# Residual block on one core: gate_up weights alone on SyncE's queue, first products one step apart, sums of h2 behind the last norm, second products out of other tiles

## The chip, the cores and the metric

One core of a Trainium2 chip runs the whole program. The metric is the device time of one execution in microseconds (us). TensorE (PE) multiplies, VectorE (DVE), ScalarE (ACT) and GpSimd (POOL) do the rest, and SyncE (SP) only issues transfers. Each engine works through its own instructions in order and waits where an operand or a buffer isn't ready. ACT, POOL and SP can each issue transfers, and an engine's transfers are issued in the order of its instructions: one that must wait holds up the ones behind it.

## What is computed

A residual block: a token mixer (attention with forgetting and a gated short convolution side by side), its output projection, then a feed-forward part. Each of the two is normed on the way in and on the way out. The sequence has 1024 rows, the model 1024 columns, the feed-forward part F = 2816 columns; all is float32.

```python
h = rmsnorm(x, norm_mix_pre)
m = mixer(h, w_in, b_f, conv_w, w_branch, w_out)   # ends in einsum(merged, w_out)
x = x + rmsnorm(m, norm_mix_post)
h = rmsnorm(x, norm_ffn_pre)
gu = einsum("bsd,df->bsf", h, w_gate_up)           # gate_up
g, u = split(gu, 2)
f = einsum("bsf,fd->bsd", silu(g) * u, w_down)     # down
x = x + rmsnorm(f, norm_ffn_post)
```

The change is at the seam between the first sum and gate_up.

## The kernel before

**Products.** A float32 operand is split into hi, a rounded copy that ACT makes, and lo, the remainder that DVE makes by a subtraction (`split`). A product `prod` of a block of weights with a block of rows is 4 steps over the inner dimension, each of three matmuls of 128x512 (hi with hi, lo with hi, hi with lo): 12 matmuls. The large products use a scheme of the Strassen kind, with seven block products instead of eight, in which sums of the blocks are made ahead (T1 to T4 of the rows, S1 to S4 of the weights).

**Output projection.** The eight row tiles of 128 go in four pairs i (PAIRS). For each, `first` and `second` were done ahead, and the loop does `p_s2`, `p_s1`, `p_s3`, `p_s4`, `p_a22`. Then `e_norm(i)` norms the result, adds the residual x (tiles `xt`, loaded by `load_xt` up to three tiles ahead), stores the sum in `x2_dram`, and norms it again for the feed-forward part. `e_turn(i)` transposes these two row tiles on PE into `um`: eight transposes of the first tile (it lies in a raw slot, or in `keep` for i = 3), then eight of the second (`tt`). The halves of `um` are split into the operands `hb[B11]` and `hb[B21]`.

**gate_up.** The columns go in 22 blocks f, each of one gate and one up block of 128 columns and seven products. For the first 11 (NPRE) the two products that need B11 and B21 alone, A11 times B11 and A12 times B21, are done early: `f_first(f)` loads a weight block (512 KB, tile `raw`), splits it, does the first product into a bank, copies it to p1, does the second into the same bank on top of it, copies that to a tile `s4`, and stores both in `pre_dram` by POOL's queue. For f = 0 `e_turn(2)` stands between the two, for f = 3 `e_turn(3)`. `h2_sums(sl)` makes T1 to T4 of a quarter of the columns of `um`: four subtractions, and four splits. It is called twice between the early blocks, and twice behind f = 4 and 5. A loop over all 22 blocks follows, in which `strassen` does the five products that are left of the first 11 and all seven of the others; `prep_rest` makes their S1 to S4, S4 by way of the tile `s4`.

**What sets the order.** The helper `InOrder` records each operation (so all have one line, 76, in the profile, and are told apart by tile names), and a scheduler orders them for each engine; `pinned` keeps some in the order of the code. Tiles come from rings: `raw` has 3 buffers, `hi` 4, `lo` 3, `s4` 1, `s4h` and `s4l` 2, `sx` 1, the tiles `c21`, `c12`, `c22` of pool `fp` 2 each; a new tile waits until the users of the buffer's last one are done. Three of the raw slots also hold the normed row tiles until they are transposed. On SP's queue stand the loads of xt, the stores to x2_dram and the loads of the gate_up weights, in one line. In the profile the bank of a product is `b` (in the order of instructions `b_` and a number, one for each block f), `x` is an operand of hb, `s` and `c` are the tiles by which results leave, `x_dram` is x2_dram.

Of the kernel before, what the change touches and what calls it, by code (L numbers as in the profile page):

```python
# [10 lines left out]
F32 = mybir.dt.float32  # L11
# [6 lines left out]
P = 128  # L18
# [4 lines left out]
NC = 512  # L23
# [16 lines left out]
NPRE = 11  # L40
# [6 lines left out]
def block_kernel(  # L47
# [16 lines left out]
    n1, n2 = slice(0, NC), slice(NC, S)  # L64
# [3 lines left out]
    class InOrder:  # L68
# [15 lines left out]
    nc = SimpleNamespace(  # L84
        **{e: InOrder(e) for e in engines}
    )
    x2d = x[0]
# [6 lines left out]
    def pool(name, bufs=1, side="left", space=None):  # L94
        kw = dict(name=name, bufs=bufs)
        if space is not DRAM:
            kw["reuse_waits"] = "tile"
        if space is not None:
            kw["space"] = space
        else:  # L100
            kw["side"] = side
        stack = ExitStack()
        ctx.callback(stack.close)
        return stack.enter_context(tc.tile_pool(**kw)), stack.close
# [4 lines left out]
    def add(o, a, b):  # L109
        nc.vector.tensor_tensor(o, a, b, op=ALU.add)  # L110

    def sub(o, a, b):
        nc.vector.tensor_tensor(o, a, b, op=ALU.subtract)
# [4 lines left out]
    def pinned(call, *names):  # L118

        was, strict[0] = strict[0], names  # L120
        call()
        strict[0] = was

    def copy(o, a):
        nc.scalar.activation(o, a, AF.Copy)
# [6 lines left out]
    def mm3(ps, a, b, start, stop, **kw):  # L132

        ah, al = a
        bh, bl = b
        nc.tensor.matmul(ps, ah, bh, start=start, stop=False, **kw)
        nc.tensor.matmul(ps, ah, bl, start=False, stop=False, **kw)
        nc.tensor.matmul(ps, al, bh, start=False, stop=stop, **kw)
# [8 lines left out]
    x2_dram = dpool.tile([S, D], F32, name="x2_dram")  # L147
# [6 lines left out]
    pre_dram = [dpool.tile([2, P, NC], F32, name=f"pre_dram{f}") for f in range(NPRE)]  # L154
# [47 lines left out]
    def z_tile(name, dt=F32, w=S):  # L202
        return zp.tile([P, S], dt, tag="z", name=name, bufs=2)[:, :w]
# [218 lines left out]
    def flat(t):  # L422
        return t.rearrange("p a b -> p (a b)")

    def kblk(t):
        return t.rearrange("p (a b) -> p a b", b=P)

    def wtile(tag, bufs, dt=F32, shape=(P, KT, P)):
        return wpool.tile(list(shape), dt, tag=tag, name=tag, bufs=bufs)

    def raw_t():
        return wtile("raw", 3)
# [7 lines left out]
    def s4_t():  # L440
        return wtile("s4", 1, F32, (P, 4, P))
# [57 lines left out]
    def bank(psp, name):  # L499
        return psp.tile([P, NC], F32, tag="mm", name=name)  # L500

    def prod(ps, w, b, first):
        (ah, al), (bh, bl) = w, b
        kw = {} if first else dict(skip_group_check=True)
        for k in range(4):
            mm3(
                ps,
                (ah[:, k, :], al[:, k, :]),
                (bh[:, k, :], bl[:, k, :]),
                first and k == 0,  # L510
                k == 3,
                **kw,
            )

    def t_(tmp, name):
        return tmp.tile([P, NC], F32, tag=name, name=name)
# [52 lines left out]
    psm, psm_close = pool("psm", 6, space=PSUM)  # L569

    def wcols(c0):
        return win[:, c0 : c0 + P]
# [304 lines left out]
    for ij, (kind, j, _, _) in enumerate(jobs):  # L877
# [8 lines left out]
        if ij < 2:  # L886
# [6 lines left out]
            w = {**w, **prep_rest(wcols(jobs[ij][3]), r1)}  # L893
            if ij == 1:
                pairs.q.append(pairs.prep(*pairs.srcs.popleft()))
            _, c12, c21, c22 = strassen(w, h1b, psm, pp, p1, mid)
        elif ij < len(jobs) - 1:
# [5 lines left out]
            c11, c12, c21, c22 = strassen(pairs.get(), h1b, psm, pp, None, mid)  # L903
        else:
            w = pairs.get()
# [3 lines left out]
            c11, c12, c21, c22 = last_pair(w)  # L909
# [288 lines left out]
    psm, psm_close = pool("psm2", 8, space=PSUM)  # L1198
# [32 lines left out]
    def both(t):  # L1231
        return t[:, 0], t[:, 1]
# [75 lines left out]
    pk, pk_close = pool("pk", 4, space=PSUM)  # L1308
    psm, psm_close = pool("psm3", 4, space=PSUM)

    wy, wy_close = pool("wy", side="right")
    fe, fe_close = pool("fe", 2)
# [11 lines left out]
    def st2(name, bufs=2):  # L1324
        return ep.tile([P, 2], F32, tag=name, name=name, bufs=bufs)

    def scale2(ssq):
        return rms_scale(ssq, None, lambda n, w: st2(n), 2)
# [5 lines left out]
    sx = wtile("sx", 1)  # L1334
# [3 lines left out]

    def load_xt(st):
        xt = ep.tile([P, D], F32, name="xt") if st % 3 == 2 else z_tile("xt")  # L1340
        nc.sync.dma_start(xt, x2d[st * P : (st + 1) * P, :])
        return xt

    xts = deque(load_xt(st) for st in range(3))
# [58 lines left out]
    def e_norm(i):  # L1403
        qa = qas[i]
        add(qa, qa, qbs[i])
        rs = scale2(qa)
        tt = keeps[i], ep.tile([P, D], F32, tag="t", name="tt", bufs=1)
        xp = [xts.popleft() for _ in range(2)]
        ssq = st2("ssq")
        for e, parts in enumerate(  # L1410
            (((slice(0, D), keeps[i]),), ((n1, b1s[i]), (n2, c22s[i])))
        ):
            for ns, c in parts:
                nc.vector.scalar_tensor_tensor(
                    tt[e][:, ns], c, rs[:, e : e + 1], gpo[:, ns], op0=ALU.mult, op1=ALU.mult
                )
            add(xp[e], xp[e], tt[e])
            rows_ = slice((2 * i + e) * P, (2 * i + e + 1) * P)
            nc.sync.dma_start(x2_dram[rows_, :], xp[e])
            nc.scalar.activation(tt[e], xp[e], AF.Square, accum_out=ssq[:, e : e + 1])  # L1420
        rs = scale2(ssq)
        for e in range(2):
            nc.vector.scalar_tensor_tensor(
                tt[e], xp[e], rs[:, e : e + 1], gpr, op0=ALU.mult, op1=ALU.mult
            )
            if 2 * i + 3 + e < ST:
                xts.append(load_xt(2 * i + 3 + e))
        turned.append(tt)

    def e_turn(i):  # L1430
        for e in range(2):
            st = 2 * i + e
            ss = slice(st * P, (st + 1) * P)
            for q in range(2):
                tp = psm.tile([P, 4, P], F32, tag="mm", name="tp")

                def turns():
                    for k in range(4):
                        kt = 4 * q + k
                        nc.tensor.transpose(  # L1440
                            tp[:, k, :], turned[i][e][:, kt * P : (kt + 1) * P], ident
                        )

                pinned(turns, "tensor")
                copy(um[:, 4 * q : 4 * q + 4, ss], tp)
# [8 lines left out]
    for k in (0, 2):  # L1454
        w = ep.tile([P, D], F32, tag="t", name="wr", bufs=1)
        cut_wo(w, ((B22, 4 + k, n2), (B22, 5 + k, n2)))

    def f_src(f):
        return wgu[:, f * P : (f + 1) * P], wgu[:, FH + f * P : FH + (f + 1) * P]

    def f_first(f, p1=None, after=None):
        w, _ = prep_first(f_src(f)[0])
        b1 = bank(psm, "b1")
        prod(b1, w["A11"], hb[B11], True)
        if after is not None:
            after()
        if p1 is None:
            p1 = t_(fp, "c21")
        copy(p1, b1)
        prod(b1, w["A12"], hb[B21], False)  # L1470
        c11 = flat(s4_t())
        copy(c11, b1)
        nc.gpsimd.dma_start(pre_dram[f][0], p1)
        nc.gpsimd.dma_start(pre_dram[f][1], c11)

    h2b11 = x_tile(1)
# [6 lines left out]
    def h2_sums(sl):  # L1483
        a = slice(sl * P, (sl + 1) * P)
        b = slice(NC + sl * P, NC + (sl + 1) * P)
        b11, b12 = um[:, 0:4, a], um[:, 0:4, b]
        b21, b22 = um[:, 4:8, a], um[:, 4:8, b]
        u, w = wtile("sx", 1), raw_t()
        sub(u[:, LO], b12, b11)
        sub(u[:, UP], b22, u[:, LO])  # L1490
        sub(w[:, LO], b22, b12)
        sub(w[:, UP], b21, u[:, UP])
        for o, t in ((T2, u[:, UP]), (T1, u[:, LO]), (T3, w[:, LO]), (T4, w[:, UP])):
            split(hb[o][0][:, :, a], hb[o][1][:, :, a], t)
# [21 lines left out]
        e_norm(i)  # L1516
    hb.append(None)
    hb += [both(x_tile(n, p)) for n, p in ((0, wx), (3, wx), (4, wy), (5, wy))]
    def p1_of(f):
        return t_(fe, "c22")  # L1520

    f_first(0, p1_of(0), lambda: e_turn(2))
    f_first(1, p1_of(1))
    h2_sums(0)
    f_first(2, p1_of(2))
    h2_sums(1)
    f_first(3, p1_of(3), lambda: e_turn(3))
    ep_close()
    fe_close()
    psm_close()  # L1530
# [1 line left out]
    psm, psm_close = pool("psm4", 8, space=PSUM)  # L1532

    hc_pool, hc_close = pool("hc")
    fp, fp_close = pool("f", 2)
    hch = hc_pool.tile([P, 4, NC], F32R, name="hch")
    hcl = hc_pool.tile([P, 4, NC], F32R, name="hcl")
    hb[B22] = hch, hcl
    for f in range(4, NPRE):
        f_first(f)  # L1540
        if f < 6:
            h2_sums(f - 2)
        if f == 6:
            for sl in range(4):
                a = slice(sl * P, (sl + 1) * P)
                b = slice(NC + sl * P, NC + (sl + 1) * P)
                split(hch[:, :, a], hcl[:, :, a], um[:, UP, b])
# [25 lines left out]
    for f in range(NF):  # L1573
        if f < NPRE:
            p1 = t_(fp, "c21")
# [164 lines left out]
    p1, c22, c11, c12 = (quarter(s_) for s_ in (4, 6, 0, 2))  # L1740
# [109 lines left out]
```

## Time and profile before

| | us |
|---|---|
| median of three runs | 1347.06 |
| the three runs | 1346.71, 1347.06, 1347.97 |
| the profiled execution, its own time | 1347.87 |
| its span | 1346.1 |
| TensorE busy in it | 1319.9 |
| VectorE busy in it | 967.7 |
| ScalarE busy in it | 560.1 |
| GpSimd busy in it | 138.4 |

The span goes from the first to the last instruction; the execution's own time is 1.8 us longer. A row of a timeline has the start, the length, the engine, the operation with its tiles (out<-in) and shape, a count (xN, a run of like instructions told in one row), and in brackets the idle time before it with what ended it. Rows of different engines overlap, and on PE an instruction starts before the one ahead of it has ended, so lengths there don't add up. A row of waits has the engine and the tile that waited, what it waited for, the sum, the number and the longest. A row of transfers has the count, the size of one, and the median time from issue to landing. A stretch has its bounds, its length, the busy time of each engine that is listed (with the number of instructions), the granted clock of TensorE (1.00 is full), the share of the transfer engines and GB/s.

### The profile page before, as it was taken

The page shows a single profiled execution, that of the slowest core. Times are in us where ns is not written, and L with a number is a line of the kernel's source. Part 1 is how long each engine was busy: PE and PEld are TensorE (multiplying, and loading weights), DVE is VectorE, ACT ScalarE, POOL GpSimd, SP SyncE. Part 2 cuts the span into 40 slices and gives each one's busy share as a digit, 9 for nine tenths or more (in the row PEclk, how much of TensorE's full clock was granted, in tenths as well). Part 3 has the DMA queues.
Part 4 walks back from the last instruction along what each step waited for, and adds up shares of the span by engine and source line. Part 5 has one row for each costly group of instructions (what it writes and reads, how often), then busy time and mean ns, then how long its engine had stood idle before and what let it go on. Part 6 is the DMA issues. An engine that isn't in the chain of part 4 may idle for free.

```text
span 1346.1 us, 18023 instructions
## 1 busy us (share of the span) xinstructions
PE 1319.9 (98%) x6705; PEld 1089.5 (81%) x6705; DVE 967.7 (72%) x1530; ACT 560.1 (42%) x896; POOL 138.4 (10%) x264
## 2 busy tenths in 40 slices
PE   9999999999999999999999999999999999999997
PEld 7978888888887778788876778888888887888886
DVE  6975678775656767686798299897767766677585
ACT  6642222243355756514577233232222323444452
POOL 0001000010112112010001212220011101000000
PEclk9999999999999999999999999999999999999999
DMA  5334444455536444466247555652333326966541
GB/s 189 119 117 133 150 113 122 136 162 152 154 117 196 158 134 159 144 231 219 77 158 239 168 180 188 187 170 89 110 116 104 110 95 248 354 241 192 160 165 63
DMA packets 189738, 212.59 MB, mean 158 GB/s; under 512 B 11585, under 2 KB 137601, under 8 KB 189650
## 3 DMA queue, kind: packets, MB, share of 16 engines
q1 hardware_dynamic: 157890, 154.50, 36.7%
q0 software_dynamic: 14864, 48.55, 9.7%
q10 hardware_dynamic: 16896, 8.39, 2.1%
q8 instruction: 52, 0.85, 0.3%
q14 instruction: 36, 0.29, 0.1%
HBM read 151.83 MB, written 59.57 MB: 157 GB/s over the span
## 4 chain that ended last, share of the span: by engine, by line
PE 54%; DVE 5%; issue 2%; DMA 2%; ACT 1%; POOL 0%; DVEq 0%; SPq 0%; POOLq 0%; ACTq 0%
PE b L76 26%; PE pd L76 15%; PE pbb L76 3%; PE pba L76 2%; PE p L76 2%; PE po L76 1%; PE tps L76 1%; PE sp L76 1%; DMA raw<-in_w_gate_up_dram 1%; PE q L76 1%; DVE x L76 1%; DVE lo L76 1%; DVE raw L76 1%; DMA tk<-in_w_down_dram 1%; DVE tt L76 0%
## 5 line engine op out<-in xcount | busy, mean ns | idle before, releaser
L76 PE MATMUL b<-x,hi 128*128 128x512 f32 x1088 | 337.3, 391 | 3.4 <-ACT hi L76 1.7
L76 PEld LDWEIGHTS b<-x,hi 128*128 128x128 f32 x1088 | 203.1, 188 | 49.3 <-ACT c L76 4.4
L76 PE MATMUL b<-x,lo 128*128 128x512 f32 x544 | 211.9, 390 | 2.0 <-DVE lo L76 2.0
L76 DVE TENSOR_TENSOR c<-c,b 128x512 f32<-128x512 f32 x199 | 135.5, 682 | 68.6 <-PE b L76 61.3
L76 DVE TENSOR_TENSOR lo<-raw,hi 128x1024 fp32r<-128x1024 f32 (+1 forms) x93 | 112.0, 1204 | 72.4 <-PE b L76 59.4
L76 ACT ACTIVATE hi<-raw 128x1024 fp32r<-128x1024 f32 (+1 forms) x100 | 101.9, 1020 | 109.6 <-PE b L76 59.9
L76 ACT ACTIVATE hi<-sx 128x1024 fp32r<-128x1024 f32 (+1 forms) x43 | 44.8, 1042 | 187.6 <-PE b L76 150.9
L76 PEld LDWEIGHTS b<-x,lo 128*128 128x128 f32 x544 | 102.1, 188 | 24.3 <-DVE lo L76 2.8
L76 DVE TENSOR_TENSOR lo<-sx,hi 128x1024 fp32r<-128x1024 f32 (+1 forms) x43 | 51.5, 1198 | 30.8 <-PE b L76 30.1
L76 DVE TENSOR_TENSOR sx<-raw 128x512 f32<-128x512 f32 x78 | 53.6, 687 | 21.3 <-DMA raw<-in_w_gate_up_dram 9.5
L76 PE MATMUL pd<-hi 128*128 128x512 f32 x160 | 62.0, 391 | 0.6 <-ACT hi L76 0.6
L76 PE MATMUL pd<-hi,lo 128*128 128x512 f32 x160 | 62.3, 389 | 0.0
L76 PE MATMUL pd<-ghi 128*128 128x512 f32 x148 | 57.6, 389 | 0.0
L76 PE MATMUL pd<-glo,ghi 128*128 128x512 f32 x148 | 57.6, 389 | 0.0
L76 PE MATMUL pd<-ghi,glo 128*128 128x512 f32 x148 | 57.6, 389 | 0.0
L76 PE MATMUL b<-hT34h,hi 128*128 128x512 f32 x136 | 53.3, 392 | 0.6 <-DVE c L76 0.4
L76 PE MATMUL b<-hT34l,hi 128*128 128x512 f32 x136 | 52.9, 389 | 0.0
L76 PE MATMUL b<-hT34h,lo 128*128 128x512 f32 x136 | 52.9, 389 | 0.0
L76 PE MATMUL b<-hT12h,hi 128*128 128x512 f32 x136 | 52.9, 389 | 0.0
L76 PE MATMUL b<-hT12l,hi 128*128 128x512 f32 x136 | 52.9, 389 | 0.0
L76 PE MATMUL b<-hT12h,lo 128*128 128x512 f32 x136 | 52.9, 389 | 0.0
L76 ACT ACTIVATE s4h<-s 128x512 fp32r<-128x512 f32 x48 | 30.1, 628 | 52.8 <-DVE s L76 42.5
(410 smaller groups left out, 3026.5 us busy)
## 6 DMA issues: line engine op xcount, KB each, us to landing
raw<-in_w_gate_up_dram SPq DMA_DIRECT2D x55, 512.0 KB, 4.2
raw<-in_w_in_dram SPq DMA_DIRECT2D x35, 512.0 KB, 5.0
a_dramS<-um POOLq DMA_DIRECT2D x44, 256.0 KB, 2.9
a_dramA<-um POOLq DMA_DIRECT2D x33, 256.0 KB, 2.7
xt<-in_x_dram SPq DMA_DIRECT2D x16, 512.0 KB, 4.4
sg<-sg_dram SPq DMA_DIRECT2D x32, 256.0 KB, 3.1
x<-wo_dram SPq DMA_DIRECT2D x16, 512.0 KB, 8.7
graw<-a_dramS SPq DMA_DIRECT2D x14, 512.0 KB, 3.6
```

Of the source, the lines that this page charges most:

```text
L76: ins = getattr(self.engine, name)(*args, **kw)
```

## The change

The loads of xt and the stores of x2_dram go from SP's queue to GpSimd's. `f_first` is cut in two: `f_begin` loads, splits, does the first product, copies and stores it; `f_end` does the second, copies and stores that. The program begins block f + 1 before it ends block f. The early four copy their first product into the halves of `sx` and two `c22` tiles, and take their banks from the pool in which the output projection had `p1`. One raw slot is passed over before f = 2. `h2_sums` is called for f = 4 to 7, all behind the last norm, and has its `w` in a z tile rather than a raw slot. From f = 4 on the second product leaves by a `c12` tile (two buffers) and not by the `s4` tile (one). The split of the B22 operand (`hch`, `hcl`) moves from f = 6 to f = 8. What is computed stays the same.

```diff
     def load_xt(st):
-        nc.sync.dma_start(xt, x2d[st * P : (st + 1) * P, :])
+        nc.gpsimd.dma_start(xt, x2d[st * P : (st + 1) * P, :])
...
-            nc.sync.dma_start(x2_dram[rows_, :], xp[e])
+            nc.gpsimd.dma_start(x2_dram[rows_, :], xp[e])
...
-    def f_first(f, p1=None, after=None):
+    begun = {}
+
+    def f_begin(f, b1, p1):
         w, _ = prep_first(f_src(f)[0])
-        b1 = bank(psm, "b1")
         prod(b1, w["A11"], hb[B11], True)
-        if after is not None:
-            after()
-        if p1 is None:
-            p1 = t_(fp, "c21")
         copy(p1, b1)
+        nc.gpsimd.dma_start(pre_dram[f][0], p1)
+        begun[f] = w, b1
+
+    def f_end(f, c11):
+        w, b1 = begun.pop(f)
         prod(b1, w["A12"], hb[B21], False)
-        c11 = flat(s4_t())
         copy(c11, b1)
-        nc.gpsimd.dma_start(pre_dram[f][0], p1)
         nc.gpsimd.dma_start(pre_dram[f][1], c11)
...
-        u, w = wtile("sx", 1), raw_t()
+        u, w = wtile("sx", 1), kblk(z_tile("w"))
...
-    def p1_of(f):
-        return t_(fe, "c22")
-
-    f_first(0, p1_of(0), lambda: e_turn(2))
-    f_first(1, p1_of(1))
-    h2_sums(0)
-    f_first(2, p1_of(2))
-    h2_sums(1)
-    f_first(3, p1_of(3), lambda: e_turn(3))
+    sx = flat(wtile("sx", 1))
+    early = [sx[:, n1], sx[:, n2], t_(fe, "c22"), t_(fe, "c22")]
+
+    def begin_early(f):
+        if f == 2:
+            raw_t()
+        f_begin(f, pk.tile([P, NC], F32, tag="p1", name="b1"), early[f])
+
+    def end_early(f):
+        f_end(f, flat(s4_t()))
+
+    begin_early(0)
+    e_turn(2)
+    begin_early(1)
+    end_early(0)
+    begin_early(2)
+    end_early(1)
+    begin_early(3)
+    e_turn(3)
+    end_early(2)
+    end_early(3)
...
-    for f in range(4, NPRE):
-        f_first(f)
-        if f < 6:
-            h2_sums(f - 2)
-        if f == 6:
+    for f in range(4, NPRE + 1):
+        if f < NPRE:
+            f_begin(f, bank(psm, "b1"), t_(fp, "c21"))
+        if f > 4:
+            f_end(f - 1, t_(fp, "c12"))
+        if f < 8:
+            h2_sums(f - 4)
+        if f == 8:
```

In the order of instructions, SP's queue from the second early weight block on (rows with - stand in the program before, rows with + in the changed one; xN is a run of N):

```order
-L76 DMA raw<-in_w_gate_up_dram 128x8x128
-L76 DMA xt<-in_x_dram 128x1024 x2
-L76 DMA x_dram<-xt 128x1024 x2
-L76 DMA xt<-in_x_dram 128x1024
-L76 DMA raw<-in_w_gate_up_dram 128x8x128
-L76 DMA x_dram<-xt 128x1024
-L76 DMA raw<-in_w_gate_up_dram 128x8x128
-L76 DMA x_dram<-xt 128x1024
-L76 DMA raw<-in_w_gate_up_dram 128x8x128 x51
+L76 DMA raw<-in_w_gate_up_dram 128x8x128 x55
```

The weights now stand in one run, with nothing else between them.

PE at the end of the first early product and `e_turn(2)`, before (`b_6760` is the bank of f = 0, `x_6185` the operand B11, `x_6552` B21, `tp` the transposes):

```order
L76 MATMUL b_6760<-x_6185,lo 128x512
L76 MATMUL b_6760<-x_6552,hi 128x512
L76 MATMUL tp<-ident,raw 128x128 x8
L76 MATMUL b_6760<-x_6552,hi 128x512
L76 MATMUL tp<-ident,tt 128x128 x8
```

and in the changed program (`b_6756` is f = 0, `b_6801` f = 1):

```order
L76 MATMUL b_6801<-x_6185,hi 128x512 x2
L76 MATMUL tp<-ident,raw 128x128 x8
L76 MATMUL b_6801<-x_6185,lo 128x512
L76 MATMUL tp<-ident,tt 128x128 x8
L76 MATMUL b_6756<-x_6552,hi 128x512 x2
```

The first product of the next block now stands between the first and the second of f = 0, and the transposes lie in it.

DVE in the last `e_norm`, from the first of the small operations that make the norm's factor to the one that applies it, before (`sx` and `raw` from `um` are subtractions of `h2_sums`, `x_6749` to `x_6752` its remainders):

```order
L76 RECIPROCAL r_6714<-sq 128x2
L76 TENSOR_TENSOR raw<-um 128x512
L76 TENSOR_TENSOR t_6718<-r_6714,va 128x2
L76 TENSOR_TENSOR raw<-um,sx 128x512
L76 TENSOR_TENSOR t_6718<-t_6718,r_6714 128x2
L76 TENSOR_TENSOR x_6750<-sx,x_6750 128x4x128
L76 TENSOR_SCALAR t_6718<-t_6718 128x2
L76 TENSOR_TENSOR x_6749<-sx,x_6749 128x4x128
L76 TENSOR_TENSOR r_6719<-r_6714,t_6718 128x2
L76 TENSOR_TENSOR x_6751<-raw,x_6751 128x4x128
L76 SCALAR_TENSOR_TENSOR keep<-keep,r_6719,gpo 128x1024
```

and in the changed program:

```order
L76 RECIPROCAL r_6714<-sq 128x2
L76 TENSOR_TENSOR t_6718<-r_6714,va 128x2
L76 TENSOR_TENSOR t_6718<-t_6718,r_6714 128x2
L76 TENSOR_SCALAR t_6718<-t_6718 128x2
L76 TENSOR_TENSOR r_6719<-r_6714,t_6718 128x2
L76 SCALAR_TENSOR_TENSOR keep<-keep,r_6719,gpo 128x1024
```

The five operations of the sums are gone from between them; they stand further down, behind the last norm's final two operations and the splits of the next weight blocks.

## The prediction

> **What bounds the kernel now.** I read the page first (the span and the busy time of each engine), then the busy time in stretches of 25 us around the changed code, then the waits of TensorE there, then the queues and engines that it waits for.
>
> ```profile
> span 1346.1 us, 18023 instructions
> PE 1319.9 (98%) x6705; PEld 1089.5 (81%) x6705; DVE 967.7 (72%) x1530; ACT 560.1 (42%) x896; POOL 138.4 (10%) x264
> ```
>
> TensorE is busy for 98% of the span, so only time in which it stands still can be won: 26.2 us in all. The stretches (length; PE busy; the other engines; clock; DMA) say where a part of it lies:
>
> ```profile
> 700.00:725.00 25.00, 21.69 (x100) 16.73 (x99) 23.80 (x43) 17.74 (x32) 3.78 (x7) 1.00 0.63 212
> ...
> 750.00:775.00 25.00, 23.22 (x102) 18.50 (x101) 7.86 (x10) 6.73 (x10) 4.87 (x9) 1.00 0.44 140
> ```
>
> DVE (third pair) is 95% busy from 700 to 725 and idle for 17 of 25 us from 750 to 775, and PE loses time in both. Cut where the program's steps end (690.3 us is where the first gate_up product starts, 792 where the first rest of a block is nearly through), PE alone:
>
> ```profile
> 690.30:733.40 43.10, 38.37 (x177) 1.00 0.58 189
> 733.40:767.50 34.10, 33.62 (x147) 1.00 0.65 213
> 767.50:792.00 24.50, 21.89 (x94) 1.00 0.46 140
> ```
>
> Idle are 4.73 + 0.48 + 2.61 = 7.8 us, at a granted clock of 1.00. Idle understates the loss, since each stop also has a tail and a restart that count as busy. The pace without stops, from two starts 30 matmuls apart, and eight transposes from the start of one block to the next:
>
> ```profile
> 765.83 0.39 PE L76 MATMUL b<-x,lo 128*128 128x512 f32 x1
> ...
> 772.63 0.39 PE L76 MATMUL b<-x,lo 128*128 128x512 f32 x1
> ```
>
> ```profile
> 719.43 1.03 PE L76 MATMUL tp<-ident,keep 128*128 128x128 f32 x8
> 720.30 1.12 PE L76 MATMUL tp<-ident,tt 128*128 128x128 f32 x8
> ```
>
> 6.80 / 30 = 0.2267 us a matmul, 0.87 us for eight transposes. The three stretches hold 418 instructions, 32 of them transposes: 386 x 0.2267 + 4 x 0.87 = 91.0 us of the 101.7. **Lost: 10.7 us, the most that this change can win there.** What ends the stops, in that window (us in total, times, longest):
>
> ```profile
> PE b L76 <- DVE c L76: 2.5, 2, 1.8
> PE b L76 <- DVE lo L76: 2.0, 2, 1.3
> PE b L76 <- ACT hi L76: 1.7, 2, 1.2
> PE b L76 <- ACT c L76: 1.4, 3, 0.7
> ```
>
> **Weights (hi, lo: 3.7 us).** hi is ACT's rounded copy of a weight block, lo DVE's remainder. SyncE's queue (start; length of the row; idle) shows why they are late:
>
> ```profile
> 681.14 0.38 SPq L76 DMA_DIRECT2D raw<-in_w_gate_up_dram  x1
> 682.49 1.57 SPq L76 DMA_DIRECT2D xt<-in_x_dram  x2
> 688.58 3.38 SPq L76 DMA_DIRECT2D x_dram<-xt  x2
> 696.79 0.33 SPq L76 DMA_DIRECT2D xt<-in_x_dram  x1
> 697.18 0.43 SPq L76 DMA_DIRECT2D raw<-in_w_gate_up_dram  x1
> 706.66 0.33 SPq L76 DMA_DIRECT2D x_dram<-xt  x1
> 707.98 0.38 SPq L76 DMA_DIRECT2D raw<-in_w_gate_up_dram  x1
> ```
>
> ```profile
> SPq L76 <- DVE xt L76: 45.0, 8, 20.4
> ```
>
> The third and fourth blocks are issued at 697.18 and 707.98, each behind a transfer of the norm that must wait for DVE (45.0 us of such waits between 655 and 815). The third lands at 704.33 and holds up ACT and then PE; the fourth's remainder waits on DVE too.
>
> ```profile
> 704.33 1.06 ACT L76 ACTIVATE hi<-raw 128x1024 fp32r<-128x1024 f32 x1 [1.26 <-DMA raw<-in_w_gate_up_dram]
> 705.44 1.22 PE L76 MATMUL b<-x,hi 128*128 128x512 f32 x4 [1.22 <-ACT hi L76]
> ```
>
> With the norm's transfers on POOL's queue a weight waits for its slot alone. By the order of the changed program the third block's slot comes free when the raw half of e_turn(1) is transposed, the fourth's when lo of the second block is done:
>
> ```profile
> 685.02 1.03 PE L76 MATMUL tp<-ident,raw 128*128 128x128 f32 x8
> ```
>
> ```profile
> 686.20 1.22 DVE L76 TENSOR_TENSOR lo<-raw,hi 128x1024 fp32r<-128x1024 f32 x1
> ```
>
> Issue is then about 686.1 and 687.5, 11.1 and 20.5 us earlier, and with the median to landing they are there at about 690.3 and 691.7:
>
> ```profile
> raw<-in_w_gate_up_dram SPq DMA_DIRECT2D x55, 512.0 KB, 4.2
> xt<-in_x_dram SPq DMA_DIRECT2D x16, 512.0 KB, 4.4
> pre_dram<-c POOLq DMA_DIRECT2D x11, 256.0 KB, 3.9
> ```
>
> Neither load is awaited by PE any more. Their hi copies now stand ahead of the norm's squares in ACT's order, which moves two copies of some 1.0 us on ACT and a remainder of some 1.1 us on DVE (each a little under its row's length, since successors overlap) in front of that chain; this is in the replay below.
>
> **First products one step apart, sums behind the norm (c on ACT: 1.4 us, and what is left of lo).** Before, PE's second product of a block stood behind ACT's copy of the first out of the same bank:
>
> ```profile
> 696.72 0.51 PE L76 MATMUL b<-x,hi 128*128 128x512 f32 x1 [0.69 <-ACT c L76]
> ```
>
> Now another block's 12 matmuls, 12 x 0.2267 = 2.72 us, lie between, longer than any of the three waits, so these go. Two operations of the sums, back to back on DVE:
>
> ```profile
> 723.77 1.29 DVE L76 TENSOR_TENSOR x<-sx,x 128x512 fp32r<-128x512 f32 x2
> ```
>
> That is a pace of about 0.60 us each. Of 16 of them between 698 and 716, ahead of the last norm, 12 leave: 7.2 us. I replayed PE, DVE and ACT by the new order with the durations of before:
>
> ```profile
> 695.44 1.29 DVE L76 SCALAR_TENSOR_TENSOR raw<-xt,r,gpr 128x1024 f32<-128x1024 f32 x1
> ```
>
> ```profile
> 716.29 1.28 DVE L76 SCALAR_TENSOR_TENSOR keep<-xt,r,gpr 128x1024 f32<-128x1024 f32 x1
> ```
>
> The first of these ends at 696.73 before. With lo of the third block (1.1) and two short operations moved in front it ends at about 698.2. PE does the first block's first product until 696.0 and ten matmuls of the next until 698.28, so e_turn(2) stalls 0 to 0.1. The second is late by 1.5 for the same reason and early by 7.2; ACT's squares between hold it back in turn, and the replay has it end at 712.63. PE has then done the first products up to the fourth block and five matmuls of the third's second: 712.4. Stall about 0.3, and 0.1 at the transposes behind it. One copy of the fifth block may cost 0 to 0.2. Together 0.7 us, and four restarts at some 0.15 (estimate: 0.51 us of that first matmul against 0.39 in a run, and the first of the next) give 1.3. The moved sums need 12 x 0.60 = 7.2 us of DVE later, beside f = 4 to 7, where PE has the first products to do and DVE is idle for 17 us of 25 soon behind: no cost; without that cover, the first rest would wait up to as long.
>
> **Second products by two c12 tiles (c on DVE: 2.5 us).** Before, all second products leave by the one s4 tile:
>
> ```profile
> 772.64 0.69 DVE L76 TENSOR_TENSOR s<-raw,sx 128x512 f32<-128x512 f32 x1 [4.33 <-DMA pre_dram<-s]
> ```
>
> ```profile
> 774.80 0.47 PE L76 MATMUL b<-hch,s4h 128*128 128x512 f32 x1 [1.78 <-DVE c L76]
> ```
>
> DVE waited 4.33 us for the store of the last of them to free s4, and everything behind it in DVE's order came late, up to the sums c: PE waits 1.8 us at 774.80 and the other 0.7 of the row above one step later. With c12 the first rest's preparation waits only for its weights, in the replay at about 744 to 750, and PE needs it at 760: both waits go, with nothing near behind them.
>
> **Transfers on POOL's queue.** Eight loads and eight stores of 512 KB leave SP and cost POOL an issue each, which no engine waits for. No row shows 512 KB on that queue. Landing is bounded by 3.9 us (256 KB there, the row of pre_dram above) and 11.3 (the slowest 512 KB group):
>
> ```profile
> tk<-in_w_down_dram SPq DMA_DIRECT2D x5, 512.0 KB, 11.3
> ```
>
> The last two loads that matter are issued in the replay at about 682.5 and 698.3, and DVE's adds want them at 690.4 and 705.1: 7.9 and 6.8 us. I take the nearest, SP's own 4.4, at no cost; 11.3 would delay DVE by 4.5. The change adds one wait: the first sx of the sums on DVE follows the stores of both first products out of the same tile, and behind it in DVE's order stand the last norm's small steps and lo of the fourth block, so e_turn(3) would be late with it. At 3.9 us to landing the stores are done by about 705 in the replay, and DVE comes to it at 706: nothing, with 1 us in hand. One rule speaks against the move. The Trainium skill, "SBUF — State Buffer", section "SBUF: two separate sides", warns that descriptors of a GpSimd-queue transfer are written by GpSimd, which is locked out while DVE runs a two-port mode; by it the loads would be late just where DVE is full, and the time would be rival C's. The trace has this neighbouring case:
>
> ```profile
> L76 POOL DMA_DIRECT2D pre_dram<-c x11 | 6.0, 542 | 113.0 <-ACT c L76 112.9
> ```
>
> These issues take 542 ns on average, some of them between 700 and 725 where DVE is 95% busy and others where it is idle; no lock is seen.
>
> **The sum.** 10.7 - 1.3 = 9.4 us less than the profiled execution: 1347.87 (the span of 1346.1 and 1.8 around it) - 9.4 = 1338.5. The median of the runs, 1347.06, lies 0.8 lower, so I say **1337.7**. A measurement of this kernel can tell about 0.2%, 2.7 us, from no change.
>
> **Rivals.**
>
> A. *The norm takes its place.* DVE is full around 700 and gets lo of two more blocks ahead of the last norm, as ACT gets their hi. If a weight lands at 7.1 us as the third did before (697.18 to 704.3), ACT's in-order queue holds the square behind it, and the chain to the last transposes is later by up to 3 us, twice (e_turn(2), e_turn(3)). For: ACT and DVE run in order, and the chain has less than 0.5 us of slack. Against: SP is free, and most land within 4.2. Gain 2.7 to 7, time 1340 to 1344.4.
>
> B. *The change doesn't do what it says:* the weights are no earlier, because slots and not the queue hold them, or because landing stretches as more transfers start together; then the first 4.7 stay and little but c goes (2.5 + 1.4 less new stops): within 2.7 us of before. Against it stands the 45.0 us. The Trainium skill, "DMA: Bandwidth & Descriptors", section "Issuing engines are not separate DMA queues", says that spreading over issuing engines saves only issue time; by it one would expect this case. But the waits above are of SP's in-order sequencer, which that sentence doesn't speak of.
>
> C. *Slower.* The xt loads on POOL's queue land so late that DVE's adds of the norm, hence its transposes, hence all second products wait. The point: 6.8 of slack + 9.4 of gain + 2.7, some 19 us to landing; at 21 us the time is 1352. Against: no 512 KB group has a median over 11.3.
>
> **Chances.** Forecast (gain 7 to 11.5, 1335.6 to 1340.1) 0.70; A 0.20; B 0.07; C 0.03. The range, 1335.6 to 1342.5, takes in the forecast and more than half of A. Faster by over 0.2%: 0.90; within: 0.07; slower: 0.03.
>
> **What would show it.** Right: the fourth weight issued near 687 on SP; no PE wait on hi or lo from 690 to 735; short waits of tp at about 698 and 712; no wait for c of 1.8 where the first rest adds its sums; about 9 us fewer in the same steps, and the same from there on. Wrong: xt landing over 8 us, DVE waiting for a DMA of xt, ACT's hi waiting for raw ahead of the norm's squares, or PE waiting for DVE keep by over 1 us.

## The result: 1.9 us, and the profile after

| | before | changed |
|---|---|---|
| median (20 runs each), us | 1347.63 | 1345.74 |
| lowest to highest | 1346.50 to 1348.95 | 1344.36 to 1347.24 |
| ratio, 95% interval | | 0.9986 (0.9979 to 0.9992) |
| the profiled execution, its span | 1347.87, 1346.1 | 1345.66, 1343.9 |

Faster by about 0.14%, where 0.7% was forecast. At 757 us of the span 7.6 us are gained (9.4 were forecast in all), and between 762 and 775 all of it is lost. First the stretches of 25 us (PE, its weight loads, DVE, ACT, POOL, clock, transfers):

```profile
700.00:725.00 25.00, 24.71 (x117) 20.01 (x116) 24.24 (x37) 20.24 (x37) 5.16 (x10) 1.00 0.72 240
725.00:750.00 25.00, 25.00 (x112) 20.70 (x111) 18.10 (x26) 14.84 (x24) 5.72 (x12) 1.00 0.59 194
750.00:775.00 25.00, 17.57 (x69) 14.00 (x68) 11.43 (x15) 5.61 (x9) 3.74 (x7) 0.86 0.53 164
```

From 700 to 725 PE is busy for 24.71 us instead of 21.69. From 750 to 775 it is busy for 17.57 instead of 23.22, and the mean clock granted there is 0.86. All of PE's waits for tiles between 690.3 and 792:

```profile
PE b L76 <- DVE c L76: 7.4, 1, 7.4
PE tp L76 <- DVE keep L76: 0.2, 1, 0.2
```

The four kinds of short stops are gone but for 0.2 us, and one long stop has come. PE's timeline around it:

```profile
762.38 0.39 PE L76 MATMUL b<-x,lo 128*128 128x512 f32 x1
770.20 1.22 PE L76 MATMUL b<-x,hi 128*128 128x512 f32 x2 [7.43 <-DVE c L76]
771.22 0.63 PE L76 MATMUL b<-x,lo 128*128 128x512 f32 x1
...
775.16 0.39 PE L76 MATMUL b<-hch,s4h 128*128 128x512 f32 x1
```

This is the first rest (the loop over all blocks, f = 0). Its products T2 and T1 are done at 762.6; the third adds onto the bank of the first and must wait until DVE has taken the first sum c out. Then its 12 matmuls take 4.96 us (770.20 to 775.16) instead of 12 x 0.2267 = 2.72. The clock in stretches of 1 us (length, PE busy, clock, transfers):

```profile
766.00:767.00 1.00, 0.00 (x0) 1.00 0.34 122
767.00:768.00 1.00, 0.00 (x0) 0.96 0.10 36
768.00:769.00 1.00, 0.00 (x0) 0.50 0.02 8
...
774.00:775.00 1.00, 1.00 (x4) 0.62 0.69 206
775.00:776.00 1.00, 1.00 (x6) 1.00 0.00 0
```

About 5 us into the stop the granted clock falls to half, and it is back some 4.6 us after the restart. DVE in the stop:

```profile
759.97 1.22 DVE L76 TENSOR_TENSOR lo<-sx,hi 128x1024 fp32r<-128x1024 f32 x1
768.13 0.69 DVE L76 TENSOR_TENSOR sx<-raw 128x512 f32<-128x512 f32 x1 [6.95 <-DMA raw<-in_w_gate_up_dram]
768.86 0.69 DVE L76 TENSOR_TENSOR raw<-raw 128x512 f32<-128x512 f32 x1
769.47 0.68 DVE L76 TENSOR_TENSOR c<-c,b 128x512 f32<-128x512 f32 x1
```

DVE is idle for 7 us: ahead of c stands sx<-raw, the first step of the third block's preparation, and it waits for a weight. That weight was issued at 760.11 and took 7.9 us (start on SP's queue; median to landing, here of this one load):

```profile
760.11 0.37 SPq L76 DMA_DIRECT2D raw<-in_w_gate_up_dram  x1
raw<-in_w_gate_up_dram SPq DMA_DIRECT2D x1, 512.0 KB, 7.9
```

Two weights and three transfers to and from pre_dram were under way together then. In the program before, s stood behind the first c and waited 4.33 us for the s4 tile; the third block's sx came after it.

Working back by 2.72 us a product, the first rest begins at about 764.8 before (774.80 less a stop of 1.78 and three products) and at about 757.2 after (762.6 less two): 7.6 us earlier. At the product with S4, 774.80 and 775.16, nothing of that is left. The 2.2 us by which the span is shorter come behind it: 1.2 us are there by 792 (the same product starts at 791.52 instead of 792.72), since the program before stops once more for c one step later (0.7 us, with its tail and restart) and the changed one doesn't; the last 1.0 us comes later, in no single stop, and no run shows its cause.

### The profile page after: what moved, and what is told of

The parts are those of the page before. It is cut to its first block, busy times and chain, and to the rows that moved or that the text cites. A ratio compares the mean times of both kernels' runs of the same rounds, so it can differ in the third digit from the quotient of the medians.

```text
span 1343.9 us, 18020 instructions
## 1 busy us (share of the span) xinstructions
PE 1319.0 (98%) x6705; PEld 1092.3 (81%) x6705; DVE 969.4 (72%) x1530; ACT 559.4 (42%) x896; POOL 147.0 (11%) x280
## 4 chain that ended last, share of the span: by engine, by line
PE 57%; DMA 2%; DVE 2%; issue 2%; ACT 1%; POOL 0%; DVEq 0%; SPq 0%; ACTq 0%; POOLq 0%
PE b L76 29%; PE pd L76 15%; PE pbb L76 3%; PE pba L76 2%; PE p L76 2%; DMA raw<-in_w_gate_up_dram 2%; PE po L76 1%; PE tps L76 1%; PE sp L76 1%; PE q L76 1%; DMA tk<-in_w_down_dram 1%; DVE lo L76 0%; DVE sx L76 0%; DVE raw L76 0%; POOL pre_dram L76 0%
```

## The experiments

All times are medians; the ratios are to the kernel before, on the same chip, with 95% intervals. ORDER, SUPPLY, DVE and STAGGER are the names that the expectations give to their theories.

**Sums of the first rest ahead of the third block's preparation** (e1, all three sums; e2, the first alone). In e2 the index is 0.

```diff
-        add(c12, p1, b2)
+        sums = [add(c12, p1, b2)]
...
-            _, g2, u1_, u2 = strassen(rest.get(), hb, psm, fp, p1)
+            if f == 1:
+                with tc.issue_after(last[0][2].ins):
+                    w = rest.get()
+            else:
+                w = rest.get()
+            _, g2, u1_, u2 = strassen(w, hb, psm, fp, p1)
```

> The changed kernel, with the preparation of the third block's rest queued on DVE behind the first three sums of the first rest; nothing else. Theory ORDER: PE's 7.4 us stop comes only from DVE's in-order queue, where the sum c that PE needs at 762.8 stands behind sx<-raw of the third block, which waits until 768.1 for its weight. Then the stop and the half clock after it go, and the time is some 9 us under the changed kernel (about 1336 to 1338). Theory SUPPLY: the weights of the first rests come no faster through three raw slots, and PE, which is early, only waits in another place, at the second or third rest; then the time stays within 3 us of the changed kernel's 1345.7.

> The same, but queued behind the first sum alone: sx<-raw of the third block now stands ahead of the second sum, which PE needs one product (2.7 us) later. ORDER: PE stops at the fourth product rather than the third, for 7.4 - 2.7 = about 4.7 us, ended by DVE c. The time is 2.5 us under the changed kernel, or up to 4.7 if so short a stop leaves the clock up (in the changed kernel the granted clock fell about 5 us into the stop). SUPPLY: no difference to the changed kernel.

Measured: e1 1343.63 us, 0.9972 (0.9963 to 0.9982); e2 1344.33, 0.9971 (0.9960 to 0.9982). Neither theory gave 2 us. In e1 DVE, the end of PE's stop, and POOL's and ACT's steps for the second products:

```profile
767.09 1.28 DVE L76 TENSOR_TENSOR c<-c,b 128x512 f32<-128x512 f32 x2 [6.07 <-issue]
```

```profile
767.83 1.22 PE L76 MATMUL b<-x,hi 128*128 128x512 f32 x2 [5.15 <-DVE c L76]
```

```profile
759.92 0.54 POOL L76 DMA_DIRECT2D c<-pre_dram  x1 [3.16 <-DMA pre_dram<-c]
760.52 0.54 POOL L76 DMA_DIRECT2D pre_dram<-c  x1
```

```profile
757.39 0.63 ACT L76 ACTIVATE s4h<-s 128x512 fp32r<-128x512 f32 x1 [4.90 <-DVE s L76]
757.93 1.04 ACT L76 ACTIVATE hi<-sx 128x1024 fp32r<-128x1024 f32 x1
758.87 0.58 ACT L76 ACTIVATE c<-b 128x512 f32<-128x512 f32 x1
```

Now c stands first, and still comes only at 767.09, with nothing ahead of it that the profile names ("issue"). The sum c is written to a c12 tile. There are two, and the first rest's takes over the one in which f = 9's second product left. That copy stood on ACT behind s4h<-s, which waited 4.9 us for the second block's preparation (758.87); its store stood on POOL behind a load (760.52). In that stretch the transfers of pre_dram took 6.2 to 7.3 us to land, so the tile comes free at about 767 (that store is issued at 760.52 and takes 6.4 us). In e2 PE stops at the third product too and not at the fourth, until the same moment: its expected 4.7 us were right in size for a wrong reason.

```profile
767.93 1.22 PE L76 MATMUL b<-x,hi 128*128 128x512 f32 x2 [4.71 <-DVE c L76]
```

So two holds seem to lie on this c, one until 768.1 (the order on DVE) and one until about 767 (the tile); e5 and e6 below test this.

**Second products by s4 again** (e3).

```diff
-            f_end(f - 1, t_(fp, "c12"))
+            f_end(f - 1, flat(s4_t()))
```

> The changed kernel, with the second products of f = 4 to 10 leaving by the one s4 tile again instead of the two c12 tiles. My prediction held c12 to be worth 2.5 us. By the order of this program DVE's first sum of the first rest stands ahead of s (which waits for the last store out of s4), and sx of the third block behind all but the last of the sums. ORDER: no stop of 7 us; s comes at about 761.5 and PE needs its product at 765; the time is 6 to 9 us under the changed kernel, so c12 costs time here. As predicted: about 2.5 us over the changed kernel. SUPPLY: within 3 us of it.

Measured: 1337.79, 0.9928 (0.9917 to 0.9940). As expected by ORDER, and 0.58% under the changed kernel: the c12 tiles cost some 8 us here. DVE at the same place:

```profile
760.82 0.69 DVE L76 TENSOR_TENSOR c<-c,b 128x512 f32<-128x512 f32 x1 [4.14 <-PE b L76]
762.87 0.69 DVE L76 TENSOR_TENSOR s<-raw,sx 128x512 f32<-128x512 f32 x1 [1.37 <-DMA pre_dram<-s]
```

c comes as soon as PE has its bank, and s waits 1.37 us for the store, where before it waited 4.33. PE loses 0.8 us to a later c.

**Useless matmuls in the stop** (e4). Added behind the first rest's sum into c22:

```diff
+            def warm():
+                for n in range(30):
+                    nc.tensor.matmul(b4, w["S1"][0][:, 0, :], hb[T1][0][:, 0, :], start=True, stop=True)
+
+            pinned(warm, "tensor")
```

> The changed kernel with 30 matmuls of no use (6.8 us, into a bank that nobody reads) between the second and the third product of the first rest, where PE stands still. If the half clock after the stop comes from the stop (PE idle), it stays at 1.00 here, and the time falls by what the slow matmuls cost after 770.2, about 2 us. If it doesn't, the time is the same; if the wait of DVE were shorter than 6.8 us, it would be slower.

Measured: 1344.02, 0.9977 (0.9967 to 0.9986). The 30 fill the stop, and the third product follows at full pace:

```profile
762.68 6.96 PE L76 MATMUL warm<-x,hi 128*128 128x512 f32 x30
769.83 0.73 PE L76 MATMUL b<-x,hi 128*128 128x512 f32 x2 [0.19 <-DVE c L76]
...
772.68 0.39 PE L76 MATMUL b<-hch,s4h 128*128 128x512 f32 x1
```

The clock is 1.00 in all stretches there, and S4's product comes at 772.68 instead of 775.16, 2.5 us earlier. The half clock is thus a cost of the stop, some 2 us on top of its 7.4; by the times alone (1.7 us, with intervals that overlap) it wouldn't be settled. The Trainium skill, "TensorE: Matmul & The Clock Gate", section "What's actually happening", says that the clock is halved after an idle window of about 3.4 us and comes back after as long a busy one. The traces agree in kind: a stop of 1.8 us left the clock up (1.00 from 767.5 to 792 before), those of 4.7 to 7.4 didn't.

**The tile and the order, one by one** (e5, e6). The second products of f = 6 to 9 leave by c22 tiles, so that c12's are free in time; e5 has all instructions where the changed kernel has them, e6 also has e1's order.

```diff
-            f_end(f - 1, t_(fp, "c12"))
+            f_end(f - 1, t_(fp, "c22" if 6 <= f - 1 < 10 else "c12"))
```

> The changed kernel, with the second products of f = 6 to 9 leaving by c22 tiles instead of c12; order and engines of all instructions stay, only the tile differs, so that the first sum c of the first rest (a c12 tile) no longer takes over the tile of f = 9. The run with the sums moved ahead of the third block's sx (c at 767.1 instead of 769.5) has left two holds on this c: A, sx of the third block ahead of it on DVE, waiting for its weight until 768.1; B, the tile, which is free when the store of f = 9's second product has landed. If both hold it at nearly the same time, lifting B alone does nothing: 1345.7, within 1 us, and the stop of 7.4 us stays. If B alone were the cause (sx only late because of something behind the same store), the stop goes and the time is near 1337.

> Both holds lifted: tiles spread as in the run before, and the third block's preparation queued behind the first three sums. A and B: the stop goes, the clock stays at 1.00, the time is 1336.5 to 1338.5, as predicted for the changed kernel and no slower than with the s4 tile (1337.8). If the weights' own supply through three raw slots bounds this stretch (SUPPLY), PE stops at the second or third rest, and the time stays over 1340. If the load of p1 from pre_dram, which the same sum needs, is what came at 767, c doesn't move.

Measured: e5 1346.21, 0.9987 (0.9978 to 0.9995); e6 1337.23, 0.9919 (0.9905 to 0.9932). With the changed kernel and e1 this is a square:

| | order as changed | sums first |
|---|---|---|
| tile taken over from f = 9 | 0.9986 | 0.9972 (e1) |
| tile free | 0.9987 (e5) | 0.9919 (e6) |

Freeing the tile alone gives nothing, the order alone 2 us (its interval just overlaps the changed kernel's; in the trace c comes 2.4 us earlier), both 9 us. This shows the two holds, and that each covers the other. In e5 the stop is still there:

```profile
PE b L76 <- DVE c L76: 7.3, 1, 7.3
```

e6's first and third sum, and the sx that no longer holds them:

```profile
762.19 0.68 DVE L76 TENSOR_TENSOR c<-c,b 128x512 f32<-128x512 f32 x1
...
767.72 0.68 DVE L76 TENSOR_TENSOR c<-c,b 128x512 f32<-128x512 f32 x1
768.59 0.69 DVE L76 TENSOR_TENSOR sx<-raw 128x512 f32<-128x512 f32 x1 [0.19 <-DMA raw<-in_w_gate_up_dram]
```

The weight comes no earlier than before, at 768.6, and PE doesn't need it: it is busy for all of 750 to 775. SUPPLY is ruled out, and so is the load of p1, which the first c needs too: that c comes at 762.19 here. e6 is the fastest kernel of the study, not separated from e3.

```profile
750.00:775.00 25.00, 25.00 (x112) 20.51 (x111) 17.19 (x24) 10.75 (x16) 4.04 (x8) 1.00 0.65 197
```

**The parts ahead of that** (e7 to e10). e7 is e3 with these two lines on SP; e8 is the kernel before with them on POOL:

```diff
-        nc.sync.dma_start(xt, x2d[st * P : (st + 1) * P, :])
+        nc.gpsimd.dma_start(xt, x2d[st * P : (st + 1) * P, :])
...
-            nc.sync.dma_start(x2_dram[rows_, :], xp[e])
+            nc.gpsimd.dma_start(x2_dram[rows_, :], xp[e])
```

> The changed kernel with the second products by s4 (1337.8), and with the loads of xt and the stores of x2_dram back on SyncE's queue: what the queue's move is worth by itself beside the staggered products and the moved sums. If the weights' place in SP's queue was the cause of the hi and lo stops (3.7 us idle before, some 5 with tails and restarts), the time is 4 to 6 us over 1337.8. If the stagger alone gives the weights enough time, it is within 1 us of it.

> The kernel before with the move of xt and x2_dram to GpSimd's queue alone. The stops on hi and lo go (3.7 us, some 5 with tails and restarts), the stops on c of ACT (1.4) stay, and so does s4: about 1342 to 1344. If the move alone does nothing because the slots hold the weights: 1347.

Measured: e7 1339.66, 0.9936 (0.9924 to 0.9949); e8 1348.32, 1.0002 (0.9993 to 1.0011). Beside the rest of the change the queue's move is worth 1.1 us by the ratios and 1.9 us by the medians, and the intervals of e3 and e7 overlap; alone it is worth nothing. PE and DVE in e8:

```profile
711.06 0.50 PE L76 MATMUL b<-x,lo 128*128 128x512 f32 x1 [2.23 <-DVE lo L76]
```

```profile
708.65 1.22 DVE L76 TENSOR_TENSOR xt<-xt,tt 128x1024 f32<-128x1024 f32 x1
709.79 1.22 DVE L76 TENSOR_TENSOR lo<-raw,hi 128x1024 fp32r<-128x1024 f32 x1
```

The third weight is issued at 688.24 instead of 697.18, but its lo stands on DVE behind the norm and the sums, without a gap, and comes at 709.79 (708.95 before). The weight was late, and it wasn't what was late last. The fourth weight isn't even issued earlier (707.98 before):

```profile
688.24 0.37 SPq L76 DMA_DIRECT2D raw<-in_w_gate_up_dram  x1
...
708.80 0.37 SPq L76 DMA_DIRECT2D raw<-in_w_gate_up_dram  x1
```

Its slot is a raw tile that `h2_sums` has as `w`, and DVE has read that only at 708.7. For this block the slot holds the weight, and not the queue.

e9 is the kernel before with the sums and the split of B22 moved and `w` in a z tile, as in the change; e10 is the same with the queue's move as well. The sums' part of the edit:

```diff
     f_first(1, p1_of(1))
-    h2_sums(0)
     f_first(2, p1_of(2))
-    h2_sums(1)
...
-        if f < 6:
-            h2_sums(f - 2)
-        if f == 6:
+        if f < 8:
+            h2_sums(f - 4)
+        if f == 8:
```

> The kernel before, with the sums of h2 (and the split of B22) moved behind the last norm as in the change, and w in a z tile; queues, f_first and s4 as before. The run with the queue's move alone gave nothing, since lo of the third block stood behind the norm and the sums on DVE though its weight was issued 9 us earlier. Theory DVE: the 7.2 us of sums ahead of the norm are what holds lo and the transposes back, so this alone takes the lo and hi stops away (3.7 us, some 5 with tails and restarts) and leaves the c stops: 1341.5 to 1344. Theory STAGGER: the gain of the staggered kernel comes from the order of the products (time for the weights and copies), and the sums alone give under 2 us: over 1346.

> The same with the queue's move too: all of the change but the staggered products and the c12 tiles. Against the staggered kernel by s4 (1337.8) the difference is the stagger's. DVE: the c stops of ACT (1.4 us, with tails and restarts some 2.5) are what is left, 1340 to 1342; the queue is worth 0 to 2 us here, as it was beside the stagger (1.9). STAGGER: over 1345.

Measured: e9 1344.57, 0.9978 (0.9968 to 0.9988); e10 1342.90, 0.9964 (0.9952 to 0.9977). PE's waits from 690 to 850, e9 and then e10:

```profile
PE b L76 <- ACT c L76: 2.8, 3, 1.1
PE b L76 <- DVE c L76: 2.2, 2, 1.5
```

```profile
PE b L76 <- DVE c L76: 2.6, 2, 1.9
PE b L76 <- ACT c L76: 2.0, 3, 0.9
```

Every stop on hi and lo is gone in both; both kernels are up to 1 us slower than theory DVE had them, and the stops on ACT's c grew (1.4 us before). But e9 doesn't separate the sums from the weights. In it the third and fourth weight are issued early too, with the norm's transfers still on SP's queue (the same in e7, at 685.91):

```profile
686.08 1.73 SPq L76 DMA_DIRECT2D raw<-in_w_gate_up_dram  x2
```

In e7 and e9 `w` is out of the raw slots, and the two loads stand ahead of the norm's stores (688.57 in e9). So e9 shows that the queue's move isn't needed for early weights, and e8 that an early weight alone doesn't help the third block. How much of e9's 0.22% is DVE's relief and how much the slots', no run shows; the queue's move on top of it (e10) brings another 0.14%, with intervals that overlap.

What is left between e10 and e3 is the staggered products, with the banks and tiles that go with them: 0.36%, some 5 us. They take away the stops on ACT's c and, as PE comes earlier and s4 is free in time, most of those on DVE's c.

## Why the prediction failed

**The replay up to the first rest held.** The sum gave these steps a gain of 6.2 us (7.5 lost in the first two stretches, less 1.3 for new stops); of the 7.6 us at 757, 0.35 were there when the first gate_up product started (689.96 instead of 690.31), so 7.25 were gained in them. The stop at the norm's keep was forecast at about 0.3 us and is 0.2; the third and fourth weight were forecast for about 686.1 and 687.5 on SP's queue, and the two loads stand in one row there:

```profile
685.84 1.79 SPq L76 DMA_DIRECT2D raw<-in_w_gate_up_dram  x2
```

The waits on hi and lo are gone. The xt loads on POOL's queue were taken at 4.4 us:

```profile
xt<-in_x_dram POOLq DMA_DIRECT2D x8, 512.0 KB, 4.5
```

So rival C had no ground, and the lock of descriptors of which the Trainium skill ("SBUF — State Buffer", section "SBUF: two separate sides") warns isn't seen in these traces; whether a DVE operation here runs in the two-port mode that it names, no row shows. Rival A didn't come either: the transposes wait 0.2 us.

**The step that failed** is this one: "With c12 the first rest's preparation waits only for its weights ... both waits go, with nothing near behind them." I took away a wait of s, and asked what the preparation of this block would wait for. I didn't ask what else would stand in front of c once s stood earlier. The order of the changed program showed it: sx of the third block ahead of the first c on DVE, and its weight in a slot that the preparation of the first two must free first. Nor did I follow the tile: c12 was the right size and had two buffers, and the first rest needs one of these at once. The runs put some 8 us on this term, where I had put a gain of 2.5; e3, which leaves only the c12 tiles out, gives 1337.8. That this is the forecast time is in part luck, since the forecast counts on these tiles; with both holds lifted (e6, 1337.2) the tiles can't be told from s4.

**A cost that had no term:** the half clock after a long stop, 2.2 us in the trace of the changed kernel, and gone in e4. A stop of 7.4 us costs some 9.6.

**The terms ahead of it were right in sum and wrong in share.** I put the stops on hi and lo (3.7 us idle) down to the queue. Alone it gives 1.0002; the sums with `w` out of the raw slots give 0.9978 and take all of these stops away, with the queue as it was. The 45.0 us of SP's waits were real, but not the price of the queue: in e7 and e9 SP still waits over 35 us for xt, and the weights are early. The text had it that lo waits on DVE too, but the sum didn't use it. The rule of "Issuing engines are not separate DMA queues" (the Trainium skill, "DMA: Bandwidth & Descriptors"), which I set aside, agrees with e8, though not for its reason: the third block's transfer did start 9 us earlier, and DVE was the later of the two; the fourth's was held by its slot.

**The chances.** The time fell into "within 0.2%", which I gave 0.07 by way of rival B. What B says, that the weights are no earlier, is not what happened (685.84 in the row above), though a slot does hold the fourth weight where the queue alone is moved (e8). So the 0.07 was met by luck. The fitting rival, a wait that takes the place of the one removed, was looked for only at the norm (A).

## What to carry to other kernels

When a wait is removed, follow the engine's own order past it: the next instruction in line may be work for a later block that waits longer, and the engine behind it waits with it. Before a result gets "a freer tile", ask who takes that tile over next and when its last transfer lands; two such holds can cover each other, so that lifting one shows nothing, and only lifting both does. A part of a change that removes a late arrival gains only if nothing else is late at the same place: test it alone, and look in the trace what else the edit has moved.

## What the runs showed of the hardware

In the changed kernel, e1 and e2 PE stopped for 7.4, 5.2 and 4.7 us. By the clock in stretches of 1 us it fell to 0.50 about 5.2, 4.7 and 3.3 us after the last matmul, and came back about 4.6, 3.0 and 5.4 us after the restart: the shortest stop had the longest slow phase. The stretches of e2 (length, PE busy, clock, transfers), and then of e1:

```profile
766.00:767.00 1.00, 0.00 (x0) 0.74 0.70 232
...
773.00:774.00 1.00, 1.00 (x5) 0.85 0.96 280
```

```profile
767.00:768.00 1.00, 0.17 (x1) 0.71 0.18 64
...
770.00:771.00 1.00, 1.00 (x4) 0.58 0.00 0
```

If the clock steps once between 1.00 and 0.50 in such a stretch, its mean tells when. By this estimate the half clock lasts from 766.5 to 773.3 in e2 (6.8 us), from 767.4 to 770.8 in e1 (3.4) and from 767.9 to 774.8 in the changed kernel (6.8). So e2's slow phase is twice e1's after a stop of nearly the same length: the 12 matmuls behind the stop take 5.3 us in e2 (767.93 to 773.22) and 4.25 in e1 (767.83 to 772.08). What such a stop costs can't be told from its length alone.

The transfers of 256 KB to and from pre_dram took 2.3 to 7.3 us to land between 740 and 775 in e1, and the weight of 512 KB that DVE waited for 7.9 us in the changed kernel, against a median of 3.7 for these weights there: with the transfer engines busy for 0.86 of their time from 760 to 766, it took about twice as long.
